# A hybrid GDN and GLA decoder trunk on one core: 32x32 blocks inverted on VectorE in 31 steps in place of 16x16 blocks in 15, decays from one magnitude, early PSUM banks in an order of their own

## The chip, the cores and the metric

The kernel runs on one core of a Trainium2 chip. TensorE (PE) multiplies matrices into PSUM, VectorE (DVE), ScalarE (ACT) and GpSimd (POOL) work elementwise, SyncE (SP) and ACT issue transfers (DMAs). Each engine takes its own instructions in order and waits on semaphores for the others. The metric is the device time of one launch in microseconds, the median over runs.

## The reference, cut to what matters

Two layers over 2048 tokens of width 1024. The first is a gated DeltaNet (GDN) with 8 heads, the second a gated linear attention (GLA) with 4 heads; each is followed by a residual sum and a LayerNorm.

```python
# GDN, per head, in chunks; gc = cumsum of the log decay within a chunk
diff  = gc[..., :, None] - gc[..., None, :]
decay = jnp.where(causal, jnp.exp(jnp.where(causal, diff, 0.0)), 0.0)
A  = jnp.where(strict, einsum('cd,sd->cs', k * beta, k) * decay, 0.0)
uw = triangular_solve(A + eye, concat([v * beta, kb * exp(gc)]))
qk = einsum('cd,sd->cs', q, k) * decay
...
def step(S, inp):                      # over the chunks
    v_new = u_n - w_n @ S
    o = qd_n @ S + qk_n @ v_new
    S = S * gl_n + kd_n.T @ v_new
...
x = layer_norm(DEEP_ALPHA * x + mixer(x), ln_g, ln_b)
```

The change touches how `decay` and the inverse of `A + eye` are made, and how the LayerNorm is staged.

## The kernel before, in words

**Units.** The tokens lie in four groups of 512 (`TG`), each group in four chunks of 128 (`NC`). A unit is one head of one group: 32 GDN units and 16 GLA units. `PHASES` (line 1178) sets their order: GDN group 0, GDN 1, GLA 0, GDN 2, GLA 1, GDN 3, GLA 2, GLA 3. For each unit four functions run (lines 1159 to 1164): `gemms` projects keys, queries, values and the gate; `preps` makes the per-chunk matrices; `chains` runs over the four chunks with the state `S`; `outs` multiplies with the output weights and, at a group's last unit, makes the LayerNorm.

**Projections.** Weights and inputs are split into a high and a low part (fp32r), and three products are summed. In the first units the raw weights (`wraw`) are split on ACT and on POOL (`split`, line 490, from `chunk`), and the pair is written back to DRAM (`wk`); later units load that pair (`wc`, nine buffers).

**A GDN preparation** (`gdn_prep`, line 798). The cumulated decays of a chunk come back from DRAM as rows on all partitions (`Gb`). For each chunk DVE forms their difference to the chunk's own column twice, bounded below by `C_LO` into `D1` and above by `C_UP` into `D2`; ACT takes two exponentials. PE transposes the keys and forms the Gram products (`psc<-kq`); DVE multiplies them with the decays, which gives `A` (in `D1`) and the query matrix (in `D2`). The inverse of the triangular 128x128 matrix is then built up:

- the 16x16 blocks on the diagonal are masked (`W2`), summed to 16 columns (`X`), written to DRAM (`blk`, issued by ACT), and read back so that every partition holds all 16 rows of its block (`Arep`, 512 KB, issued by SP);
- 15 steps on DVE invert all blocks at once, each a product (`Xt<-Arep,X`) and a subtraction (`X<-X,Xt`), the second needing the first and the next step both;
- the blocks are spread to `Tm` and transposed to `U`;
- 16 to 32, 32 to 64 and 64 to 128 are joined on PE, each by one set of matmuls with `A` (`psc<-U,D`) and one with the inverse so far (`psc<-W,Tm`). The join to 32 is made on full 128x128 operands, the later ones on the blocks alone;
- ACT scales the result into `Uf`, which the chain's second product uses (`psh<-Rt,D`).

Each step of the inversion and the lines of this join read as follows (lines 853 to 868, cut):

```python
for q in range(15, 0, -1):
    v.tensor_tensor(xt[:, :, :q], R[:, q, :, :q], X[:, :, q:q + 1].broadcast_to([P, NC, q]), ALU.mult)
    v.tensor_tensor(X[:, :, :q], X[:, :, :q], xt[:, :, :q], ALU.subtract)
...
```

**What sets the order.** The code does not run as it is written. `Recorder.note` records every operation with its dependencies and a rank; `Recorder.place` then lays all of them out with a cost for each (`cost`), a lag until its result can be used, and one clock per engine: of what could go, the lowest rank goes first (chain, preparation, output, projection, LayerNorm, setup), then the earlier recorded. What comes out is each engine's fixed order of instructions; all of them have one line, 364, in the profile. A tile gets its buffer when its first operation is placed, and tiles of one name and one rank get theirs in the order in which they were recorded. So the PSUM banks `psc` of a preparation, three in all, are handed out in recorded order: first the transposes and Gram products of a unit, then those of its joins, then those of the next unit. A dependent operation was taken to be ready 160 ns after the one before it had ended (`LAG`, `SLACK`).

**LayerNorm** (`layer_norm`, line 1145). For each chunk: statistics, then for each half of the 1024 columns two DVE instructions with the gain and the bias (`gb`, four buffers of their own), then a store.

Of the kernel before, what the change touches and what calls it, by code (L numbers as in the profile page):

```python
# [27 lines left out]
BIG = 1.0e30  # L28
# [4 lines left out]
C_ID, C_TRI, C_LO, C_UP, C_BLK, C_LV = 0, 1, 2, 3, 4, 5  # L33
# [3 lines left out]
def shape_constants(np):  # L37
    i = np.arange(P)[:, None]
    j = np.arange(P)[None, :]
    c = np.zeros((P, N_CST, P), np.float32)  # L40
    c[:, C_ID] = i == j
    c[:, C_TRI] = i <= j
    c[:, C_LO] = np.where(j < i, 0.0, BIG)
    c[:, C_UP] = np.where(j >= i, 0.0, -BIG)
    c[:, C_BLK] = (i // 16) == (j // 16)
    for n, s in enumerate(LEVELS[:5]):
        c[:, C_LV + n] = (i // (2 * s) == j // (2 * s)) & (i % (2 * s) < s) & (j % (2 * s) >= s)
    return c.reshape(P, N_CST * P)
# [75 lines left out]
class Recorder:  # L124
# [11 lines left out]
    def note(self, engine, key, name, args, kw, also):  # L136
# [9 lines left out]
        for v in views:  # L146
# [19 lines left out]
            if t not in op.views:  # L166
                op.views.append(t)
                t.left += 1
        for v in also:
# [14 lines left out]
    def cost(self, op, dst, every):  # L184
# [14 lines left out]
        elif key == "d":  # L199
# [3 lines left out]
            if tag == "Arep":  # L203
                op.cost, op.lag = 720, REP_LAG
# [30 lines left out]
    def place(self):  # L235
# [47 lines left out]
        while len(placed) < len(self.ops):  # L283
# [48 lines left out]
            for u in op.users:  # L332
                u.ready = max(u.ready, now + cost if u.deps[op] else end + (100 if u.key == "t" else 0) + SLACK)
# [33 lines left out]
class Recorded:  # L367
# [3 lines left out]
    def __getattr__(self, name):  # L371
        def call(*args, also=(), **kw):
            key = "a" if self.key == "s" and name == "dma_start" else self.key
            self.recorder.note(self.engine, key, name, args, kw, also)
# [3 lines left out]
LAG = 60  # L378
DMA_LAG, REP_LAG, SLACK = 3500, 9000, 100
# [4 lines left out]
def trunk(ctx, tc, x, xT, w_in1, conv, a_log, dt_bias, nw1, w_out1, w_in2, gk_up, gk_b, nw2, w_out2,  # L384
# [51 lines left out]
    id16 = T("id16", [P, 16])  # L436
# [18 lines left out]
    def setup():  # L455
# [11 lines left out]
        v.tensor_reduce(id16[:], ident.rearrange("p (a b) -> p b a", b=16), mybir.AxisListType.X, ALU.add)  # L467
# [34 lines left out]
    def transposes(dst, src_of, n, w=P):  # L502
        for i in range(n):
            pe.transpose(dst[:, i, :], src_of(i), cst[:w, C_ID, :w])
# [239 lines left out]
    def gdn_logits(G, gi):  # L744
# [29 lines left out]
        gc, gl = T("gc", [P, 2, H1, NC], 2), T("gdec", hn, 2)  # L774
# [3 lines left out]
        s.activation(gl[:], gl[:], AF.Exp)  # L778
        eg = T("eg", [P, 2, H1, NC], 2)
# [7 lines left out]
        G.update(beta=beta, gc=gc, gdec=gl, eg=eg, rows=rows)  # L787
# [10 lines left out]
    def gdn_prep(u):  # L798
        h, G = u.h, u.G
        beta, gc, eg = G["beta"][:, h, :], G["gc"][:, 0, h, :], G["eg"]  # L800
# [4 lines left out]
        for n in range(NC):  # L805
            v.scalar_tensor_tensor(D1[:, n], Gb[:, n], gc[:, n:n + 1], C(C_LO), ALU.subtract, ALU.max)
            v.scalar_tensor_tensor(D2[:, n], Gb[:, n], gc[:, n:n + 1], C(C_UP), ALU.subtract, ALU.min)
        s.activation(D1[:], D1[:], AF.Exp, scale=-1.0)
        s.activation(D2[:], D2[:], AF.Exp)
        s.activation(Gb[:], Gb[:], AF.Exp)  # L810
        kq = u.kq
        qd = T("qd", [P, NC, P], 2)
        v.tensor_tensor(qd[:], kq[:, 1], Gb[:], ALU.mult)
        ss, r, qn = small("ss", 2 * NC), small("rr", NC), small("qn", NC)
        kd = T("kd", [P, NC, P], 2)
        for m in range(2 if u.by_tok else 1):
            d = PS("c", [P, NC, P])
            transposes(d, lambda n: kq[:, m, n], NC)
# [13 lines left out]
        for n in range(0, NC, 2):  # L832
            d = PS("c", [P, 2, 2 * P])
            for i in range(2):
                mm(d[:, i, :], kq[:, 0, n + i], kq[:, :, n + i, :])
            for i in range(2):
# [4 lines left out]
        Tm, U, W2 = T("Tm", [P, NC, P]), T("U", [P, NC, P]), T("W2", [P, NC, P])  # L841
        X = T("X", [P, NC, 16])
        v.tensor_tensor(W2[:], A[:], bc(C(C_BLK), 1, NC), ALU.mult)
        v.tensor_reduce(X[:], W2[:].rearrange("p n (b j) -> p n j b", j=16), mybir.AxisListType.X, ALU.add)
        blk = T(f"blk_{u.at}", [P, NC * 16], p=dr)
        acts.dma_start(blk[:], flat(X[:]))
        R = T("Arep", [P, 16, NC, 16])
        sync.dma_start(R[:].rearrange("p s n j -> p (s n j)"),
                            bc(blk[:].rearrange("(b s) n -> b (s n)", b=8), 1, 16))
        X = T("X", [P, NC, 16])  # L850
        xt = T("Xt", [P, NC, 16])
        g.tensor_copy(X[:], bc(id16[:], 1, NC))
        for q in range(15, 0, -1):
            v.tensor_tensor(xt[:, :, :q], R[:, q, :, :q], X[:, :, q:q + 1].broadcast_to([P, NC, q]), ALU.mult)
            v.tensor_tensor(X[:, :, :q], X[:, :, :q], xt[:, :, :q], ALU.subtract)
        v.tensor_tensor(Tm[:].rearrange("p n (b j) -> p n b j", j=16), bc(X[:], 2, 8),
                        bc(C(C_BLK).rearrange("p (b j) -> p b j", j=16), 1, NC), ALU.mult)
        v.transpose(flat(U[:]), flat(Tm[:]))
        Uh, Wh = later_half(U[:], 16), halves(W2[:, :, :P // 2], 16)
        d = halves(PS("c", [P, NC, P // 2]), 16)  # L860
        for n in range(NC):
            mm(d[:, n], A[:, n], Uh[:, n])
        v.tensor_tensor(Wh, d, bc(later_half(C(C_LV + 4), 16), 1, NC), ALU.mult)
        d = halves(PS("c", [P, NC, P // 2]), 16)
        for n in range(NC):
            mm(d[:, n], Tm[:, n], Wh[:, n])
        v.tensor_tensor(Uh, Uh, d, ALU.subtract)
        v.transpose(flat(Tm[:]), flat(U[:]))
# [21 lines left out]
    def gla_prep(u):  # L890
# [3 lines left out]
        ab, xm = T("Gb", [P, TG]), T("W2", [P, TG])  # L894
# [12 lines left out]
        near = T("Arep", [P, NC, 2 * P])  # L907
# [186 lines left out]
    def outs(u):  # L1094
# [9 lines left out]
        if end:  # L1104
            wo = {e: load_wo(spec, ("xh", "xl")) for e, spec in enumerate(u.wo_specs())}
            gb = load_gb(u)
        for e, n in [(e, n) for n in range(NC) for e in range(2)] if end else [(e, n) for e in range(2) for n in range(NC)]:
# [3 lines left out]
            if final and not n and not end:  # L1111
                rec.rank = R_LN
                gb = load_gb(u)
                rec.rank = R_OUT
# [7 lines left out]
            if final:  # L1122
                if not end:
# [95 lines left out]
```

## Time and profile before

| | us |
|---|---|
| median of 3 runs | 3043.78 (3040.22 to 3046.16) |
| the profiled execution | 3042.14 |
| its span, first to last instruction | 3040.3 |
| PE busy | 2961.3 (97%) |
| PE weight loads busy | 2470.7 (81%) |
| DVE busy | 2099.5 (69%) |
| ACT busy | 1183.6 (39%) |
| POOL busy | 508.9 (17%) |

An engine's busy time is the time in which it had an instruction under way; 1.8 us of the execution lie outside the span. A group's row gives line, engine, operation, what it writes and from what, shapes and count, then busy time and mean of one in ns, then the idle time before it and what ended that. A wait's row gives who waited, for whom, us in total, times, and the longest. TensorE's granted clock was 0.994 in the mean. An fp32 matmul stands as two records.

### The profile page before, as it was taken

The page shows a single profiled execution, that of the slowest core. Times are in us where ns is not written, and L with a number is a line of the kernel's source. Part 1 is how long each engine was busy: PE and PEld are TensorE (multiplying, and loading weights), DVE is VectorE, ACT ScalarE, POOL GpSimd, SP SyncE. Part 2 cuts the span into 40 slices and gives each one's busy share as a digit, 9 for nine tenths or more (in the row PEclk, how much of TensorE's full clock was granted, in tenths as well). Part 3 has the DMA queues.
Part 4 walks back from the last instruction along what each step waited for, and adds up shares of the span by engine and source line. Part 5 has one row for each costly group of instructions (what it writes and reads, how often), then busy time and mean ns, then how long its engine had stood idle before and what let it go on. Part 6 is the DMA issues. An engine that isn't in the chain of part 4 may idle for free. (4 is left out here: it accounts for less than half of the span.)

```text
span 3040.3 us, 47938 instructions
## 1 busy us (share of the span) xinstructions
PE 2961.3 (97%) x16684; PEld 2470.7 (81%) x16684; DVE 2099.5 (69%) x4730; ACT 1183.6 (39%) x3009; POOL 508.9 (17%) x848
## 2 busy tenths in 40 slices
PE   8999999999999999999999999999999999999997
PEld 6777778778888888878888888888888888888886
DVE  6877787866776696576677668448667676655755
ACT  5444444533323455332332344333333334433431
POOL 5443333410000233210000000001001000000000
PEclk9999999999999999999999999999999999999998
DMA  6666666764556557785454556667454545766754
GB/s 189 179 202 193 212 219 197 248 216 139 149 154 174 173 181 255 237 268 165 143 150 150 178 177 199 220 222 257 136 154 147 159 150 177 253 198 218 236 177 146
DMA packets 455778, 577.33 MB, mean 190 GB/s; under 512 B 40640, under 2 KB 387008, under 8 KB 443504
## 3 DMA queue, kind: packets, MB, share of 16 engines
q1 hardware_dynamic: 441520, 556.37, 58.3%
q10 hardware_dynamic: 14016, 17.90, 2.0%
q8 instruction: 131, 2.15, 0.3%
q14 instruction: 111, 0.91, 0.1%
HBM read 446.94 MB, written 127.21 MB: 189 GB/s over the span
## 5 line engine op out<-in xcount | busy, mean ns | idle before, releaser
L364 PE MATMUL psg<-xh,wc 128*128 128x512 f32 x3936 | 1337.8, 407 | 19.9 <-DMA wc<-wk 6.9
L364 PEld LDWEIGHTS psg<-xh,wc 128*128 128x128 f32 x3936 | 735.0, 189 | 181.2 <-POOL wc L364 9.6
L364 PE MATMUL psg<-xl,wc 128*128 128x512 f32 x1968 | 799.5, 407 | 0.3
L364 PE MATMUL pso<-wo,oth 128*128 128x512 f32 x1472 | 489.5, 406 | 12.2 <-DVE y L364 12.1
L364 PEld LDWEIGHTS psg<-xl,wc 128*128 128x128 f32 x1968 | 372.3, 189 | 75.4 <-DVE xl L364 1.9
L364 DVE SCALAR_TENSOR_TENSOR y<-pso,z,y 128x512 f32<-128x512 f32 x368 | 274.8, 747 | 182.0 <-PE pso L364 171.2
L364 POOL TENSOR_TENSOR wc<-wraw,wc 128x256 fp32r<-128x256 f32 (+1 forms) x336 | 288.6, 875 | 428.0 <-ACT wc L364 383.5
L364 DVE SCALAR_TENSOR_TENSOR acc<-pb,taps,acc 128x512 f32<-128x512 f32 x384 | 302.9, 793 | 53.9 <-ACT acc L364 49.9
L364 PEld LDWEIGHTS pso<-wo,oth 128*128 128x128 f32 x1472 | 262.6, 189 | 71.1 <-DVE y L364 21.1
L364 PE MATMUL pso<-wo,otl 128*128 128x512 f32 x736 | 292.8, 398 | 0.0
L364 PE MATMUL psg<-wc,xh 128*128 128x256 f32 (+1 forms) x1344 | 267.9, 291 | 8.4 <-ACT wc L364 3.9
L364 PEld LDWEIGHTS psg<-wc,xh 128*128 128x128 f32 x1344 | 216.0, 189 | 20.1 <-ACT wc L364 4.7
L364 ACT ACTIVATE th<-psg 128x512 f32<-128x512 f32 (+1 forms) x170 | 94.6, 572 | 302.7 <-PE psg L364 297.9
L364 PE MATMUL psg<-wc,xl 128*128 128x256 f32 (+1 forms) x672 | 190.2, 289 | 0.0
L364 ACT CAST wc<-wraw 128x256 fp32r<-128x256 f32 (+1 forms) x336 | 126.5, 405 | 103.1 <-DMA wraw<-in_w_in 86.0
L364 PEld LDWEIGHTS pso<-wo,otl 128*128 128x128 f32 x736 | 138.7, 188 | 29.9 <-DVE otl L364 1.1
L364 ACT COPY pb<-psg 128x512 f32<-128x512 f32 x128 | 74.8, 584 | 214.0 <-PE psg L364 202.5
L364 ACT ACTIVATE D<-D 128x512 f32<-128x512 f32 x160 | 98.1, 628 | 127.6 <-DVE D L364 121.2
L364 POOL COPY halo<-pb 128x3 f32<-128x3 f32 x128 | 36.8, 287 | 638.8 <-ACT pb L364 637.0
L364 DVE SCALAR_TENSOR_TENSOR sg<-th,psg 128x512 f32<-128x512 f32 (+1 forms) x106 | 67.0, 633 | 110.4 <-ACT th L364 100.9
L364 POOL TENSOR_SCALAR z<-ssq 128x4 f32<-128x4 f32 x44 | 16.3, 370 | 752.9 <-ACT junk L364 728.2
L364 ACT ACTIVATE sq<-psc 128x256 f32<-128x256 f32 x172 | 65.5, 382 | 163.3 <-PE psc L364 161.6
(192 smaller groups left out, 4608.0 us busy)
## 6 DMA issues: line engine op xcount, KB each, us to landing
wc<-wk SPq DMA_DIRECT2D x856, 256.0 KB
wo<-wok SPq DMA_DIRECT2D x70, 1024.0 KB
wk<-wc SPq DMA_DIRECT2D x272, 256.0 KB
wraw<-in_w_in SPq DMA_DIRECT2D x336, 128.0 KB
wok<-wo SPq DMA_DIRECT2D x24, 1024.0 KB
wc<-wk SPq DMA_DIRECT2D x80, 272.0 KB
Arep<-blk SPq DMA_DIRECT2D x32, 512.0 KB
woraw<-in_w_out SPq DMA_DIRECT2D x48, 256.0 KB
```

What stands on the lines that cost most here:

```text
L364: tc.keep_in_program_order(op.call(*[real(a) for a in op.args], **{k: real(a) for k, a in op.kw.items()}))
```

## The change

What it does:

- The diagonal blocks are 32x32: 31 steps of two instructions on DVE for 15, and the join from 16 to 32 on PE goes away, with its two DVE instructions, its mask and one transpose on DVE. ACT copies the blocks to `X0` in place of DVE's mask and sum. The block is written whole (`blk`) and as its first 16 columns (`blkq`), and read back in two transfers: rows 16 to 31 (1 MB), and rows 0 to 15 as far as they are needed (512 KB).
- The decays come from one magnitude: ACT takes `Abs(Gb - gc)` once per chunk (bias from a negated copy `ngc`) and one exponential for both uses; a product with the triangle makes `D2` from it. DVE's eight bounded differences per unit go.
- The preparation's first part (transposes, Gram products) has a rank of its own, `R_EARLY`, behind the preparation's. Its PSUM banks are so handed out in an order of their own, and it can be placed ahead of the joins of the unit before.
- In `place`, an operation of DVE that needs one of DVE is ready 35 ns after that one has ended (`DRAIN`). The lag of `Arep` is counted from 8500 ns and its size.
- LayerNorm takes the statistics of all four chunks first, then the first half of the columns of each, then the second. Its gains and biases are loaded half by half, after the first statistics, into buffers that the raw output weights (`woraw`) or the inputs (`xraw`) use otherwise.

The diff's core:

```diff
-    c[:, C_LO] = np.where(j < i, 0.0, BIG)
-    c[:, C_UP] = np.where(j >= i, 0.0, -BIG)
-    c[:, C_BLK] = (i // 16) == (j // 16)
+    c[:, C_BLK] = (i // 32) == (j // 32)
...
-                u.ready = max(u.ready, now + cost if u.deps[op] else end + (100 if u.key == "t" else 0) + SLACK)
+                u.ready = max(u.ready, now + cost if u.deps[op] else end - LAG + DRAIN if u.key == op.key == "v" else
+                              end + (100 if u.key == "t" else 0) + SLACK)
...
         for n in range(NC):
-            v.scalar_tensor_tensor(D1[:, n], Gb[:, n], gc[:, n:n + 1], C(C_LO), ALU.subtract, ALU.max)
-            v.scalar_tensor_tensor(D2[:, n], Gb[:, n], gc[:, n:n + 1], C(C_UP), ALU.subtract, ALU.min)
+            s.activation(D1[:, n], Gb[:, n], AF.Abs, bias=ngc[:, n:n + 1])
         s.activation(D1[:], D1[:], AF.Exp, scale=-1.0)
-        s.activation(D2[:], D2[:], AF.Exp)
         s.activation(Gb[:], Gb[:], AF.Exp)
+        v.tensor_tensor(D2[:], D1[:], bc(C(C_TRI), 1, NC), ALU.mult)
...
+        rec.rank = R_EARLY
...
         A = D1
...
-        v.tensor_tensor(W2[:], A[:], bc(C(C_BLK), 1, NC), ALU.mult)
-        v.tensor_reduce(X[:], W2[:].rearrange("p n (b j) -> p n j b", j=16), mybir.AxisListType.X, ALU.add)
-        blk = T(f"blk_{u.at}", [P, NC * 16], p=dr)
-        acts.dma_start(blk[:], flat(X[:]))
-        R = T("Arep", [P, 16, NC, 16])
-        sync.dma_start(R[:].rearrange("p s n j -> p (s n j)"),
-                            bc(blk[:].rearrange("(b s) n -> b (s n)", b=8), 1, 16))
+        rec.rank = R_PREP
+        own = T("X0", [P, 32 * NC])
+        for r0 in range(0, P, 32):
+            r = slice(r0, r0 + 32)
+            s.copy(own[r].rearrange("p (j n) -> p n j", n=NC), A[r, :, r])
+        late, early = (T(f"{k}_{u.at}", [P, 32 // m * NC], p=dr) for m, k in ((1, "blk"), (2, "blkq")))
+        acts.dma_start(late[:], own[:])
+        acts.dma_start(early[:], own[:, :16 * NC])
+        R = T("Arep", [P, 3 * 16 * 16 * NC])
+        n = 16 * 32 * NC
+        sync.dma_start(R[:, :n], bc(late[:].rearrange("(b s) n -> b (s n)", b=4)[:, n:], 1, 32))
+        sync.dma_start(R[:, n:], bc(early[:].rearrange("(b s) n -> b (s n)", b=4)[:, :n // 2], 1, 32))
...
-        for q in range(15, 0, -1):
-            v.tensor_tensor(xt[:, :, :q], R[:, q, :, :q], X[:, :, q:q + 1].broadcast_to([P, NC, q]), ALU.mult)
-            v.tensor_tensor(X[:, :, :q], X[:, :, :q], xt[:, :, :q], ALU.subtract)
+        for q in range(31, 0, -1):
+            at = (q - 16) * 32 * NC if q >= 16 else n + q * 16 * NC
+            row = R[:, at:at + q * NC].rearrange("p (j n) -> p j n", n=NC)
+            v.tensor_tensor(xt[:, :q], row, bc(X[:, q], 1, q), ALU.mult)
+            v.tensor_tensor(X[:, :q], X[:, :q], xt[:, :q], ALU.subtract)
...
-        for n in range(NC):
-            mm(d[:, n], A[:, n], Uh[:, n])
-        v.tensor_tensor(Wh, d, bc(later_half(C(C_LV + 4), 16), 1, NC), ALU.mult)
-        d = halves(PS("c", [P, NC, P // 2]), 16)
-        for n in range(NC):
-            mm(d[:, n], Tm[:, n], Wh[:, n])
-        v.tensor_tensor(Uh, Uh, d, ALU.subtract)
-        v.transpose(flat(Tm[:]), flat(U[:]))
...
+        if u.last and not end:
+            rec.rank = R_LN
+            for e in range(2):
+                rec.after = stats[0][0].of.given
+                gb = load_gb(u, [e])
+                rec.after = None
+                for n in range(NC):
+                    layer_norm(u, n, ys[n], e, *stats[n], gb)
...
-R_CHAIN, R_PREP, R_OUT, R_GEMM, R_LN, R_SETUP = range(6)
+R_CHAIN, R_PREP, R_EARLY, R_OUT, R_GEMM, R_LN, R_SETUP = range(7)
```

How the instructions move, at three places. On PE, the joins of the first unit; `psg<-xh,wc` is a projection of a later unit, `U` and `W` the operands of the joins, `D` holds `A`. Before:

```order
L364 MATMUL psg_111<-xh_127,wc_137 128x512
L364 MATMUL psc_168<-U_200,D_0_178 128x64 x4
L364 MATMUL psg_110<-xh_124,wc_143 128x512
L364 MATMUL psg_110<-xl_132,wc_143 128x512
L364 MATMUL psg_110<-xh_124,wc_143 128x512
L364 MATMUL psg_111<-xh_128,wc_138 128x512
L364 MATMUL psg_111<-xl_136,wc_138 128x512
L364 MATMUL psc_169<-W_0_201,Tm_199 128x64 x4
```

And now:

```order
L364 MATMUL psg_109<-xh_126,wc_138 128x512
L364 MATMUL psc_167<-U_201,D_0_179 32x32 x8
L364 MATMUL psg_109<-xh_127,wc_137 128x512
L364 MATMUL psg_109<-xl_135,wc_137 128x512
L364 MATMUL psg_109<-xh_127,wc_137 128x512
L364 MATMUL psc_168<-W_0_202,Tm_200 32x32 x8
```

The two runs of four 128x64 matmuls are gone, and the first join is that on 32x32 blocks.

Also on PE, the transposes (`cst,kq`) and Gram products (`kq` 128x256) of the second unit, whose keys and queries are `kq_116`. Before they stand behind the first unit's last join (`W,Tm` 64x64):

```order
L364 MATMUL psg_109<-xh_122,wc_140 128x512
L364 MATMUL psg_109<-xl_130,wc_140 128x512
L364 MATMUL psc_169<-W_0_201,Tm_199 64x64 x4
L364 MATMUL psc_168<-cst_63,kq_116 128x128 x4
L364 MATMUL psg_109<-xh_122,wc_140 128x512
L364 MATMUL psc_169<-kq_116 128x256 x2
L364 MATMUL psh_215<-Rt_216,D_0_178 128x256
```

Now they stand here, more than a hundred rows ahead of that join:

```order
L364 MATMUL psg_109<-xh_126,wc_138 128x512
L364 MATMUL psg_109<-xh_127,wc_139 128x512
L364 MATMUL psc_168<-cst_63,kq_116 128x128 x4
L364 MATMUL psc_167<-kq_116 128x256 x2
L364 MATMUL psg_109<-xl_135,wc_139 128x512
L364 MATMUL psg_109<-xh_127,wc_139 128x512
```

The second unit's products have moved from behind the first unit's joins to before its inversion.

On DVE, steps of the inversion in the third unit, from its first on, before, with other work of DVE between: `acc` is the short convolution, `otl` and `sq` belong to the outputs.

```order
L364 TENSOR_TENSOR X_202<-X_202,Xt_205 128x4x15
L364 SCALAR_TENSOR_TENSOR acc_156<-pb_152,taps_65,acc_156 128x512
L364 TENSOR_TENSOR otl_212<-og_214,oth_210 128x512
L364 TENSOR_TENSOR sq_232<-psc_167,cst_63 128x512
L364 TENSOR_TENSOR Xt_205<-Arep_204,X_202 128x4x14
L364 SCALAR_TENSOR_TENSOR acc_156<-pb_152,taps_65,acc_156 128x512
L364 TENSOR_TENSOR X_202<-X_202,Xt_205 128x4x14
L364 SCALAR_TENSOR_TENSOR acc_156<-pb_152,taps_65,acc_156 128x512
```

And now, from the third of 31 steps on (`Rt` and `og` belong to the chain of the unit before):

```order
L364 TENSOR_TENSOR og_217<-psc_168,sg_158 128x2x128
L364 TENSOR_TENSOR X_207<-X_207,Xt_208 128x116
L364 SCALAR_TENSOR_TENSOR Rt_219<-psh_218,s_1_199,vt_114 128x256
L364 TENSOR_TENSOR Xt_208<-Arep_206,X_207 128x112
L364 TENSOR_TENSOR X_207<-X_207,Xt_208 128x112
L364 TENSOR_TENSOR Xt_208<-Arep_206,X_207 128x108
L364 TENSOR_TENSOR X_207<-X_207,Xt_208 128x108
L364 TENSOR_TENSOR Xt_208<-Arep_206,X_207 128x104
```

The steps stood singly with other work between; now they stand in pairs and longer runs, and the chain of the unit before runs beside them.

## What the change will do to the time

> **What bounds the kernel now.** First the page's busy shares, then the same by stage (one group of 512 tokens is eight GDN units, one per head; GLA units lie between). The columns are stretch, length, then busy us and instructions of PE, PEld, DVE, ACT, POOL, the granted clock, DMA share and rate.
>
> ```profile
> PE 2961.3 (97%) x16684; PEld 2470.7 (81%) x16684; DVE 2099.5 (69%) x4730; ACT 1183.6 (39%) x3009; POOL 508.9 (17%) x848
> ```
> ```profile
> 0.00:640.00 640.00, 606.11 (x3227) 485.62 (x3228) 498.59 (x1050) 304.06 (x832) 260.01 (x374) 0.99 0.66 206
> 1360.00:1800.00 440.00, 439.25 (x2426) 362.84 (x2425) 300.94 (x744) 147.82 (x392) 35.39 (x90) 1.00 0.52 160
> 2100.00:2540.00 440.00, 440.00 (x2456) 364.24 (x2455) 300.60 (x749) 151.91 (x402) 35.81 (x92) 1.00 0.53 163
> ```
>
> The late GDN stages (1360 to 1800, 2100 to 2540) have PE busy 439.25 and 440.00 of 440 us: PE sets their length. The first stage (0 to 640) has 33.9 us of idle PE, with DVE at 498.59 of 640 (78%) and POOL at 260.01. What PE waited for, first there, then from 1360 to 1800:
>
> ```profile
> PE pso L364 <- DVE y L364: 8.1, 11, 1.9
> PE psg L364 <- DVE acc L364: 7.2, 7, 2.7
> PE psg L364 <- POOL wc L364: 3.9, 9, 1.2
> ```
> ```profile
> PE psg L364 <- DVE sg L364: 0.8, 1, 0.8
> ```
>
> 19.2 us of the first stage's waits end on DVE or POOL; in the later stage 0.8 us in all does, and no wait for weights is there. So work taken from PE shortens the kernel, and DVE is what can take some back, early on.
>
> Then one unit's preparation, in the timeline (start, length):
>
> ```profile
> 2322.34 0.33 ACTq L364 DMA_DIRECT2D blk<-X  x1
> 2327.34 0.62 SPq L364 DMA_DIRECT2D Arep<-blk  x1
> 2335.93 0.22 DVE L364 TENSOR_TENSOR Xt<-Arep,X 128x60 f32<-128x60 f32 x1
> ...
> 2357.07 0.17 DVE L364 TENSOR_TENSOR Xt<-Arep,X 128x4 f32<-128x4 f32 x1
> ```
> ```profile
> 2369.74 0.68 PE L364 MATMUL psc<-W,Tm 64*64 64x64 f32 x8
> 2370.35 0.65 PE L364 MATMUL psc<-cst,kq 128*128 128x128 f32 x4
> ...
> 2371.93 0.59 PE L364 MATMUL psh<-Rt,D 128*128 128x256 f32 x2
> ...
> 2379.68 0.33 ACTq L364 DMA_DIRECT2D blk<-X  x1
> ```
>
> The last level (2369.74) is followed at once by the next unit's transposes (2370.35) and by the chain that uses the result (2371.93); the next unit's blocks are written at 2379.68, 57.3 us after this unit's. The preparations run one behind the other.
>
> **The change, part by part.** The sum is made against the profiled execution: 3042.14 us, its span 3040.3. The median of the runs shown is 1.6 us above it.
>
> (a) PE loses the level that joined 16 to 32: four matmuls by A and four by the inverse, in every one of 32 units, two records each. Two places, and what starts behind them:
>
> ```profile
> 797.61 1.00 PE L364 MATMUL psc<-U,D 128*128 128x64 f32 x8
> 798.42 0.71 PE L364 MATMUL pso<-wo,oth 128*128 128x512 f32 x2
> ...
> 799.66 1.00 PE L364 MATMUL psc<-W,Tm 128*128 128x64 f32 x8
> 800.47 0.48 PE L364 MATMUL pso<-wo,otl 128*128 128x512 f32 x1
> ...
> 801.80 0.59 PE L364 MATMUL psc<-U,D 128*32 128x32 f32 x16
> ```
>
> From start to next start a run of eight takes 0.81 us, its 1.00 us being modelled to an end that overlaps the next. I take the starts: 2 x 0.81 x 32 = 51.8 us; by the durations it would be 64, which would count the overlap. Nothing is added on PE. Since its stages are full, this is on the path: -51.8. The level's latency, 4.2 us (797.61 to 801.80), goes from the preparation too.
>
> (b) DVE loses these, and gets 62 inversion instructions a unit for 30:
>
> ```profile
> L364 DVE SCALAR_TENSOR_TENSOR D<-Gb,gc,cst 128x128 f32<-128x128 f32 x256 | 82.6, 369 | 4.7 <-PE psh L364 3.7 <-DMA Gb<-gcT 0.9
> ...
> L364 DVE TENSOR_REDUCE X<-W 128x64 f32<-128x512 f32 x32 | 33.0, 1032 | 0.3
> ...
> L364 DVE STREAM_TRANSPOSE Tm<-U 128x512 f32<-128x512 f32 x32 | 22.7, 709 | 0.8
> ...
> L364 DVE TENSOR_TENSOR W<-D,cst 128x512 f32<-128x512 f32 x32 | 22.4, 699 | 0.1
> ...
> L364 DVE TENSOR_TENSOR W<-psc,cst 128x256 f32<-128x256 f32 x32 | 13.5, 421 | 24.0 <-PE psc L364 23.7
> L364 DVE TENSOR_TENSOR U<-U,psc 128x256 f32<-128x256 f32 x32 | 13.4, 419 | 23.3 <-PE psc L364 23.2
> ```
>
> Removed per unit: 8 x 0.369 + 1.032 + 0.709 + 0.699 + 0.421 + 0.419 = 6.2 us. Added: one 512-wide product with the triangle, 0.7 us by the row of W<-D. The inversion's price differs by stage; these rows hold its products Xt alone (stretch, length, DVE busy and count):
>
> ```profile
> 0.00:640.00 640.00, 80.19 (x270) 0.99 0.66 206
> 2100.00:2540.00 440.00, 45.36 (x240) 1.00 0.53 163
> ```
>
> That is 0.297 us each early and 0.189 us late; the subtractions I price alike. The mean width doubles from 32 to 64 elements, and 56 elements cost 0.05 us in the rows above (0.22 at 60, 0.17 at 4), so 0.03 us each is added. Late: 62 x 0.219 = 13.6 us for 30 x 0.189 = 5.7, so with the rest +2.4 us a unit; in stages that have 140 us of 440 without DVE work, and PE hardly waits for it, I cost this at nothing. Early (nine units): 62 x 0.327 = 20.3 for 8.9, +5.9 a unit, 53 us together. DVE would be busy 552 of 640 - 9 x 1.6 = 625 us, 88% for 78%. Why the early ones are dearer:
>
> ```profile
> 442.78 3.09 POOL L364 TENSOR_TENSOR wc<-wraw,wc 128x256 fp32r<-128x256 f32 x4 [3.35 <-ACT wc L364]
> ...
> 444.58 0.66 DVE L364 TENSOR_TENSOR Xt<-Arep,X 128x52 f32<-128x52 f32 x1
> ...
> 445.97 0.21 DVE L364 TENSOR_TENSOR Xt<-Arep,X 128x48 f32<-128x48 f32 x1
> ```
>
> While POOL splits weights, a step takes 0.66 us, and 0.21 us as soon as it has stopped. The Trainium skill, SBUF — State Buffer, section "SBUF: two separate sides", has a rule that speaks against this change: a vector instruction with two SBUF inputs and a GpSimd instruction that reads SBUF exclude each other for a whole instruction. By it the steps would be hit in proportion to POOL's share of the stretch; 260 of 640 us at 0.45 us a hit is an estimate of 0.18 us per step, 25 us a unit for my 20, and 42 us more of DVE in the stage.
>
> What of these 53 us PE sees no row shows. From below: nothing, since steps are not what PE waits for above (y, acc and wc are). From above: the stage's idle DVE time halves, 141 to 73 us; if the 19.2 us of waits grow as it shrinks, they become 37, +18. Both ends are equally near, so I take +9.
>
> (c) ACT loses one exponential of 512 and gets four magnitudes of 128 and four copies of 32x128 blocks, and another write is issued:
>
> ```profile
> L364 ACT ACTIVATE D<-D 128x512 f32<-128x512 f32 x160 | 98.1, 628 | 127.6 <-DVE D L364 121.2 <-DVE lnmv L364 4.0 <-PE psg L364 2.1
> ...
> L364 ACT ACTIVATE D<-U,brk 128x128 f32<-128x128 f32 x128 | 40.9, 391 | 0.9
> ```
>
> At 0.39 us for each of the eight, 0.63 back and 0.33 for the issue: +2.8 us a unit on an engine busy 39%. Nothing; its cover is ACT's free 60%, and if the copies came late the inversion would start 1.6 us later.
>
> (d) Arep grows from 512 KB to 1.5 MB in two DMAs. Before, 8.6 us went from issue (2327.34) to the first step. Three times that, 26 us, bounds the whole from above, but the first steps need only the first megabyte. On SP the second DMA waits for its block's write, and weight loads are queued behind both. SP's own waits:
>
> ```profile
> SPq L364 <- PE psg L364: 1130.2, 637, 8.9
> ```
>
> SP mostly waits for buffers that PE frees, so loads go out early, and no weight was waited for from 1360 to 1800. Nothing, with 2 us a unit (64 us) as the far end if that lead is eaten.
>
> (e) The early PSUM banks in an order of their own, and vector steps placed closer: the next unit's transposes and Gram products no longer stand behind this unit's last level. That takes the longer inversion off the row of preparations: 13.6 - 5.7 = 7.9 us longer, 4.2 us of level gone. It may also free some early waits: 0, at best the whole 19.2 us.
>
> (f) LayerNorm in halves: the instruction counts stay, the gains and biases land in buffers shared with weights, and their issue waits for the first statistics, with the next unit's loads behind it on SP. Seven groups with a wait of a microsecond would be 7 us; I take 0, by the same lead.
>
> Sum: 3042.1 - 51.8 + 9 = 2999.3; with the 1.6 us to the median, 3001 us.
>
> **The rivals.**
> - *The waits do not grow* (0.34): PE saves its 51.8 us and the freed order saves some early waits, as y and acc are short steps that a vector engine with 12% to spare still serves. Against it: DVE at 88%. 2980 to 2992 us; all 19.2 us saved would be 2971.
> - *Half-late inversions* (0.13): the early steps make PE wait 2 to 4 us a unit, 18 to 36 us: 3010 to 3028.
> - *The inversion becomes the early bound, slower* (0.05): the steps cost 0.327 - 0.219 = 0.108 us more than in quiet, 62 of them 6.7 us a unit, and if PE's in-order queue reaches the next level before them each time, nine units lose 60 us: 3052. It outweighs the saving from 5.8 us a unit on. For it: steps now stand in pairs without other work between. Against: before, 3.2 us of the same excess a unit left no wait for U among the early waits.
> - *Weights late behind Arep* (0.04): from 1.6 us of PE wait a unit on there is no gain; at 2 us, 3054. Against it the SP row.
> - *PE's busy time is no bound, no gain* (0.04): the preparations' row sets the 57.3 us, and what PE loses becomes idle: 3042. The Trainium skill, Perfetto Trace Analysis, section "Identifying the Most-Contended Engine", holds that matmul busy time misjudges headroom and asks for the share of the weight loads; here that is 364.24 of 440 us. Against it: a run of 0.81 us is followed at once by the next start, and hardly a wait is left in the late stages (0.8 us) that an earlier operand would shorten.
>
> **The numbers.** The forecast, 2993 to 3010 us, has 0.40. A measurement of this kernel can tell about 0.2% (6 us) from no change. Slower by more: 0.05, of the inversion rival 0.03 and of the weights rival 0.02, the rest of both ending below 3038. Same: the no-gain case, 0.04. Faster: what is left, 0.91. For 8 in 10 the range takes in the forecast, nearly all of the first two rivals and with them the unknowns of (d) and (f): 2975 to 3026.
>
> **What would show it.** In the profile after: no psc 128x64 matmuls by U and Tm; PE still 440 of 440 in late stages, now some 13 us shorter per group; Xt near 0.33 us early and 0.22 us late; DVE near 88% before 630 us; PE's early waits on y and acc near 30 us. An early wait of psc for U or W, or of psg for wc behind Arep, would prove a rival; PE idle in the late stages would prove the reasoning wrong from its start.

## The result and the profile after

The change makes the kernel slower: 3476.39 us (median of 4 runs, 3468.62 to 3481.28) against 3042.49 in the same rounds, a ratio of 1.1424 with an interval of 1.1410 to 1.1439. The forecast was 3001 us. The profiled execution took 3474.92 us, with a span of 3472.7 and a granted clock of 0.933 in the mean.

The page's busy shares of the changed kernel:

```profile
PE 2992.4 (86%) x16172; PEld 2464.3 (71%) x16172; DVE 2207.5 (64%) x5374; ACT 1263.2 (36%) x3233; POOL 506.4 (15%) x848
```

PE ran 512 matmul records fewer. They are those of the join to 32, which is gone as forecast; a group of the joins has the forms 32 and 64 alone:

```profile
L364 PE MATMUL psc<-W,Tm x768: 191/191/367, 132.3 to 2969.5; 32*32 32x32 f32 x128, 64*64 64x64 f32 x64
```

PE was yet busy 31 us longer, and its idle time went from 79.0 us (3040.3 - 2961.3) to 480.3 (3472.7 - 2992.4). These two make the 432 us by which the span grew. By stage (stretch, length, then PE, PEld, DVE, ACT, POOL, the granted clock, DMA share, rate):

```profile
0.00:640.00 640.00, 504.04 (x2473) 394.88 (x2474) 415.36 (x983) 268.62 (x729) 211.99 (x304) 0.90 0.55 174
1360.00:1800.00 440.00, 384.03 (x2140) 319.91 (x2139) 280.48 (x660) 166.78 (x426) 79.56 (x124) 0.95 0.65 208
2100.00:2540.00 440.00, 397.82 (x2263) 339.56 (x2262) 271.35 (x646) 153.34 (x360) 27.94 (x57) 0.95 0.62 200
```

PE was to stay at 440 of 440 in the late stages and DVE to come near 88% in the first. Neither holds: DVE has 65% there (415 of 640). No engine is the bound, so the waits must tell. PE's, then one row of ACT's and one of DVE's (us in total, times, longest):

```profile
PE psg L364 <- DMA wc<-wk: 204.9, 25, 19.9
PE psg L364 <- ACT wc L364: 55.0, 7, 14.4
PE psh L364 <- DVE S L364: 51.4, 12, 9.5
PE pso L364 <- DVE y L364: 38.9, 18, 9.8
PE psh L364 <- ACT wt L364: 31.5, 7, 16.0
PE psh L364 <- DVE Rt L364: 23.5, 2, 14.0
```
```profile
ACT wc L364 <- DMA wraw<-in_w_in: 191.0, 42, 19.6
```
```profile
DVE Xt L364 <- DMA Arep<-blk: 173.8, 22, 11.4
```

Two chains come out of one place. PE waits 204.9 us for loaded weights, and 55.0 for ACT, which itself stands on raw weights not yet loaded. The waits that end on DVE (S, y, Rt) are no work of DVE's: it stands at the first step of an inversion 22 times until `Arep` lands, and what is queued behind that step on its engine waits too.

One unit in the timeline (start, length; in brackets the idle time before and what ended it):

```profile
1065.93 0.33 ACTq L364 DMA_DIRECT2D blk<-X  x1
...
1068.87 0.56 SPq L364 DMA_DIRECT2D Arep<-blk  x1
...
1069.53 0.55 SPq L364 DMA_DIRECT2D Arep<-blkq  x1
...
1070.70 16.37 SPq L364 DMA_DIRECT2D wc<-wk  x4
...
1077.40 0.40 PE L364 MATMUL psg<-xh,wc 128*128 128x512 f32 x1
...
1094.57 0.80 PE L364 MATMUL psg<-xh,wc 128*128 128x512 f32 x1 [16.78 <-DMA wc<-wk]
```
```profile
1101.46 0.28 DVE L364 TENSOR_TENSOR Xt<-Arep,X 128x124 f32<-128x124 f32 x1
```

SP issued the weights that PE lacks at 1070.70, 7 us before PE ran out: the lead that the prediction counted on was there. They came 24 us later. The trace has 16 semaphore updates for this load, one for each part that landed: twelve by 1076.17, the last four at 1090.04, 1091.68, 1093.72 and 1094.53. The four late ones of `Arep`'s second load stand at 1089.37, 1091.01, 1093.05 and 1093.84, each 0.7 us ahead of one of those. So a quarter of the weights went behind `Arep`, part by part. SP was held as well: its third issue of weights behind `Arep` (1072.98) took 9.28 us, the fourth 4.76, where in e1 below none took over 1.6. What the DMA engines did while only `Arep` was under way, from the windows of three kernels (here with PE alone: PE busy, clock, DMA share, rate), the changed kernel first, then the kernel before, then e1 below:

```profile
1076.50:1079.50 3.00, 1.30 (x6) 1.00 0.27 74
```
```profile
2269.10:2271.10 2.00, 2.00 (x12) 1.00 0.50 134
```
```profile
1625.00:1628.00 3.00, 3.00 (x15) 1.00 1.06 232
```

The changed kernel moves the three times larger tile with a quarter of the 16 engines, where the kernel before used half of them. The source of the load has its blocks outermost: eight of 16 rows before, four of 32 now. The Trainium skill, DMA: Bandwidth & Descriptors, section "Why a DMA increments its semaphore by 16 and not by 1", says that the outermost size that is not 1 sets on how many engines a transfer is spread, the largest number up to 16 that divides it on both sides. By that eight and four are what one should have expected, and the shares of 0.50 and 0.27 agree.

### The profile page after: what moved, and what is told of

It reads as the page before. It is cut to its first block, busy times and chain, and to the rows that moved or that the text cites. A ratio compares the mean times of both kernels' runs of the same rounds, so it can differ in the third digit from the quotient of the medians.

```text
span 3472.7 us, 47799 instructions
## 1 busy us (share of the span) xinstructions
PE 2992.4 (86%) x16172; PEld 2464.3 (71%) x16172; DVE 2207.5 (64%) x5374; ACT 1263.2 (36%) x3233; POOL 506.4 (15%) x848
## 5 line engine op out<-in xcount | busy, mean ns | idle before, releaser
L364 PE MATMUL psg<-xh,wc 128*128 128x512 f32 x3936 | 1365.7, 414 | 261.2 <-DMA wc<-wk 195.5
L364 PEld LDWEIGHTS psg<-xh,wc 128*128 128x128 f32 x3936 | 753.4, 193 | 439.3 <-DMA wc<-wk 204.8
L364 PE MATMUL psg<-xl,wc 128*128 128x512 f32 x1968 | 813.1, 414 | 0.2
L364 PE MATMUL pso<-wo,oth 128*128 128x512 f32 x1472 | 500.7, 414 | 40.7 <-DVE y L364 38.9
L364 PEld LDWEIGHTS psg<-xl,wc 128*128 128x128 f32 x1968 | 380.9, 194 | 78.9 <-DVE xl L364 1.5
L364 DVE TENSOR_TENSOR Xt<-Arep,X 128x124 f32<-128x124 f32 (+30 forms) x992 | 235.8, 238 | 196.9 <-DMA Arep<-blk 173.8
L364 DVE TENSOR_TENSOR X<-X,Xt 128x124 f32<-128x124 f32 (+30 forms) x992 | 234.7, 237 | 23.7
L364 DVE SCALAR_TENSOR_TENSOR S<-S,eg,psh 128x256 f32<-128x256 f32 x128 | 61.2, 478 | 173.2 <-PE psh L364 172.8
```

What stands on the lines that cost most here:

```text
L364: tc.keep_in_program_order(op.call(*[real(a) for a in op.args], **{k: real(a) for k, a in op.kw.items()}))
```

## The experiments

Three theories. **Width**: on four engines `Arep` takes long, and the weights, spread over all 16, wait for their share on these four. **Volume**: 1.5 MB in place of 0.5 is too much however spread. **Placement**: the early rank, or a planner that was told too short a lag, puts weights behind `Arep`. Times stand against the kernel before on the same chip, 3041 to 3043 us.

**e1, full width.** Each load as four, one for each 32 partitions:

```diff
-        sync.dma_start(R[:, :n], bc(late[:].rearrange("(b s) n -> b (s n)", b=4)[:, n:], 1, 32))
-        sync.dma_start(R[:, n:], bc(early[:].rearrange("(b s) n -> b (s n)", b=4)[:, :n // 2], 1, 32))
+        for part, src in ((R[:, :n], late[:].rearrange("(b s) n -> b (s n)", b=4)[:, n:]),
+                          (R[:, n:], early[:].rearrange("(b s) n -> b (s n)", b=4)[:, :n // 2])):
+            for b in range(4):
+                sync.dma_start(part[b * 32:(b + 1) * 32, :], src[b:b + 1, :].broadcast_to([32, src.shape[1]]))
```

> The changed kernel, with each of its two Arep loads issued as four, one per block of 32 partitions, so that the slowest dimension of each source is the 32 copies and no longer the 4 blocks; bytes, steps and ranks stay. Width theory (the load runs on 4 of the 16 DMA engines, busy share 0.25 in the trace, and weights queue behind it on those): the load lands within 8 us, the gaps of 10 to 17 us go, 2985 to 3020 us. Volume theory (1.5 MB in place of 512 KB is what holds the weights up): still over 3300 us. Placement theory (the new ranks and lags put DVE and SP in front of rows that cannot be there yet): still over 3300 us.

3036.1 us, ratio 0.9983 (0.9971 to 0.9994). With this one edit the whole loss is gone, 440 us, and bytes and steps are what they were: width is shown. Of 936 weight loads, 96 took over 10 us from issue to landing in the changed kernel, none here; the two loads of `Arep` took 20 and 25 us there (medians), 6 and 7 for each part here. Its page, two stages and four of PE's waits:

```profile
PE 2927.2 (96%) x16172; PEld 2416.5 (80%) x16172; DVE 2211.9 (73%) x5374; ACT 1261.3 (42%) x3233; POOL 510.3 (17%) x848
```
```profile
0.00:640.00 640.00, 595.75 (x3021) 469.45 (x3022) 516.81 (x1218) 326.30 (x892) 264.52 (x376) 0.98 0.71 217
1360.00:1800.00 440.00, 430.27 (x2331) 350.92 (x2331) 326.63 (x915) 167.93 (x450) 33.48 (x85) 0.99 0.63 184
```
```profile
PE psg L364 <- DMA wc<-wk: 26.8, 14, 5.2
PE pso L364 <- DVE y L364: 11.8, 18, 1.6
PE psg L364 <- ACT acc L364: 10.6, 9, 2.9
...
PE psc L364 <- DVE U L364: 4.9, 5, 2.7
```

This is the kernel that the prediction had in mind, but at 3036, not 3001, and above the 2985 to 3020 of the width theory too; that is taken up by e5 and those after it.

**e2, the kernel before on four engines.** Its 512 KB as two loads of four blocks each:

```diff
-        sync.dma_start(R[:].rearrange("p s n j -> p (s n j)"),
-                       bc(blk[:].rearrange("(b s) n -> b (s n)", b=8), 1, 16))
+        for k in range(2):
+            sync.dma_start(R[k * 64:(k + 1) * 64].rearrange("p s n j -> p (s n j)"),
+                           bc(blk[k * 64:(k + 1) * 64, :].rearrange("(b s) n -> b (s n)", b=4), 1, 16))
```

> The kernel before, with its 512 KB Arep load issued as two of 4 blocks each in place of one of 8 blocks; bytes, steps and placement nearly as before. Width theory: the DMA busy share in the load falls from about 0.5 to 0.25, the load takes about twice as long (9 to 10 us from its first to its last packet, for 4.5), weights come later and the steps start 4 to 5 us later: 3070 to 3200 us. Volume theory and placement theory: no more bytes and no other placement, 3035 to 3055 us.

3056.26 us, ratio 1.0049 (1.0029 to 1.0068). The load did go narrow. A window with little but this load under way (PE busy, clock, DMA share, rate):

```profile
890.50:893.50 3.00, 3.00 (x15) 1.00 0.28 101
```

The loss is less than width expected: a quarter of the engines costs 15 us where 512 KB go over them, and 440 where 1.5 MB do. It takes both, the narrow transfer and the larger tile.

**e3 and e4, placement.** `R_EARLY` made the same as `R_PREP`; and `REP_LAG` 22000 for 8500:

> The changed kernel with the early part of the preparation back in the preparation's own rank, so that PSUM banks are handed out in recorded order as before. Width theory and volume theory: over 3400 us, the load is as slow as it was. Placement theory, if the early rank is what did it: below 3150 us.

> The changed kernel, with the planner told that Arep's rows come 22 us and their size later in place of 8.5 us and their size; the transfers are as they were. Placement theory (the too short lag makes DVE wait in its queue for rows): DVE's waits for Arep go and the time falls below 3060 us. Width theory: DVE's waits for Arep go, but the weights behind it stay late, 3200 to 3450 us with PE still waiting over 100 us for wc. Volume theory: as width.

3619.55 us, ratio 1.1896 (1.1865 to 1.1927), and 3526.99, 1.1595 (1.1567 to 1.1623). Both slower than the change itself, e4 also than any of its expectations. Placement is out: without the early rank it is worse, and a planner that is told of the slow load gains nothing. In e4 DVE never waits for `Arep` any more, and PE's waits for `S` fall from 51.4 to 1.4 us, but those for weights rise to 280.1. So the late weights alone are enough for the loss; DVE need not stand for it.

**e7, issued by ACT.** Both loads on ACT's queue (`acts.dma_start` for `sync.dma_start`), still four blocks outermost:

> The changed kernel with both loads of the repeated rows issued by ACT's queue in place of SP's, still on four engines. If the weights lose their time by standing behind these loads in SP's own queue (queue), they pass them now: most of the 440 us goes, 3050 to 3150. If they lose it because the four engines that carry the repeated rows are shared by all queues (engines), a weight load needs those four too, and 250 us or more stays: 3290 to 3480. The first step's wait for the repeated rows stays at 25 us or more in both.

3469.86 us, ratio 1.1401 (1.1379 to 1.1423): the loss stays. Two of its waits:

```profile
PE psg L364 <- DMA wc<-wk: 121.2, 38, 10.9
```
```profile
DVE Xt L364 <- DMA Arep<-blk: 236.7, 24, 14.7
```

PE waits less for weights (204.9 in the changed kernel), DVE more for the repeated rows (173.8), and the time is the same. SP is free now: 4 of its weight issues took over 2 us, 59 in the changed kernel. Yet 102 weight loads were over 10 us under way, for 96, and the repeated rows took 21 and 27 us from issue to landing (medians). So it is not SP's queue but the four engines that both need.

**e8, the kernel before on all 16.** Its load as eight of 16 partitions each.

> The kernel before with its load of the repeated rows cut into eight DMAs of 16 partitions, so that all 16 engines carry its 512 KB. Width: the 10.6 us of waits for weights shrink a little, 3034 to 3042, ratio 0.997 to 1.000. If eight engines were wide enough for 512 KB: no change, 3040 to 3043. If seven more issues a unit on SP cost something: above 3045.

3046.18 us, ratio 1.0015 (1.0004 to 1.0026): no gain, if anything a loss. Eight engines were wide enough for 512 KB; whether the seven more issues cost the 5 us was not tested.

Now the 35 us between e1 and the forecast. The busy and idle time of PE in the profiled executions, worked out from span and busy time of each page:

| | time of the runs, us | PE busy | PE idle |
|---|---|---|---|
| before | 3041 | 2961.3 | 79.0 |
| e13, join left out | 2994.6 | 2908.2 | 78.9 |
| e9, few bytes, few steps | 3020.3 | 2918.6 | 94.6 |
| e1, full width | 3036.1 | 2927.2 | 108.2 |
| after | 3476.4 | 2992.4 | 480.3 |

(Of e13 and e9 the busy times are in the rows below; the idle time is the span less these: 2987.1 and 3013.2.)

```profile
PE 2908.2 (97%) x16172; PEld 2414.3 (81%) x16172; DVE 2064.9 (69%) x4634; ACT 1184.2 (40%) x3009; POOL 513.5 (17%) x848
```
```profile
PE 2918.6 (97%) x16172; PEld 2416.3 (80%) x16172; DVE 1987.8 (66%) x4350; ACT 1264.0 (42%) x3233; POOL 501.5 (17%) x848
```

**e5, e6, e9: bytes and steps.** e5 loads four late and eight early rows of each block (`R[:, :n // 4]`, and `n // 4` more), e6 runs `range(15, 0, -1)` for `range(31, 0, -1)`, e9 does both; all on e1.

> e1_full_width with a third of the bytes: of each block only four late rows and eight quarter rows are loaded (512 KB a unit in place of 1.5 MB, still one DMA for each 32 partitions), and the steps read these rows again and again, so it leaves out the other rows of the inverse; the number and the shapes of the steps stay. Volume: the waits of the matmuls for weights (wc<-wk 26.8 us in e1_full_width, 10.6 before) fall to about 10 us, and what follows them too: 3036 goes to 3008 to 3022, near the forecast. DVE load (the early steps themselves make PE wait): the time stays at 3032 to 3038 and the waits for y, acc and U stay. If both hold part, 3022 to 3032.

> e1_full_width with 15 of the 31 steps (it leaves out the 16 widest), all 1.5 MB loaded as before. 32 DVE instructions of about 0.3 us a unit go, some 9 us a unit, 300 us of DVE in all. DVE load: PE's waits for DVE (y 11.8, acc 5.2, U 4.9, kq 4.1 us in e1_full_width) shrink, 3008 to 3022. Volume: the time stays within 6 us of e1_full_width, 3030 to 3040, and the waits for weights stay near 27 us.

> e5_third_of_bytes and e6_half_the_steps in one kernel: 512 KB of repeated rows a unit on all engines, and 15 of the 31 steps (it leaves out the 16 widest steps, and most rows of the rest). Neither volume nor DVE load is then above the kernel before. If each of the two alone made up for the other in e5 and e6 (either-or): most of the 42 us comes through, 3000 to 3015. If neither is the cause, and the residue is the order of the work or ACT's part (order/ACT): 3030 to 3045 again.

3037.12 us, ratio 0.9989 (0.9979 to 0.9999); 3044.33, 1.0018 (1.0008 to 1.0028); 3020.3, 0.9932 (0.9918 to 0.9947). Neither alone gives anything (e6 is even 8 us slower than e1), both together 16 us. So volume alone and DVE load alone both fell, and "either-or" holds for a third of what it forecast. In e5 the weights were waited for less, and other waits came up:

```profile
PE pso L364 <- DVE y L364: 14.6, 20, 2.7
PE psg L364 <- DMA wc<-wk: 14.4, 9, 3.6
PE psg L364 <- ACT acc L364: 11.3, 9, 3.5
```

In e1 these were 11.8, 26.8 and 10.6 us (above). (For the kernel before, PE's waits for weights are 9.5 us in the trace, where the expectations have 10.6.) Why one of the two is enough to hold the other's gain was not found.

**e13, the join left out of the kernel before**, with its eight matmuls and their vector work, nothing in its place.

> The kernel before with the join of 16 to 32 left out and nothing put in its place (eight matmuls and their vector work a unit go; blocks of 16 in place of 32 are inverted, so the result lacks the join). PE bound as the prediction had it: the whole 51.8 us come through, 2984 to 2996, perhaps some more since DVE gets lighter too. If waits for weights and vector work come up as PE gets lighter (a second bound close behind): 3005 to 3030. PE no bound: 3036 to 3043.

2994.55 us, ratio 0.9846 (0.9831 to 0.9860), 46.6 us less. PE busy falls by 53.1 us and its idle time does not move (table), in an execution that was the fastest of the five: what PE sheds comes through, as the prediction reckoned.

**e15, the LayerNorm in halves alone** on the kernel before, and **e17**, on e1, its halves ranked `R_OUT` for `R_LN`.

> The kernel before with only the LayerNorm in halves, its gains and biases in the weights' buffers and issued behind the first statistics. The prediction put 0, at worst 7 us: 3040 to 3049. If it takes back a good part of the saving: 3049 to 3065.

> e1_full_width with the halves of the LayerNorm ranked as the output products in place of behind the projections. If what the halves cost is that they come late and hold the weights' buffers: 3022 to 3032. If it is the wait on SP's queue for the statistics: 3034 to 3045.

3054.65 us, ratio 1.0037 (1.0026 to 1.0047): 13 us lost by the medians, 8 to 14 by the interval, more than the 7 that were forecast as the worst. e17 is slower still, 3065.01, 1.0073 (1.0060 to 1.0086), beyond both its expectations. That the halves cost is shown; by what is not, since the profiled execution of e15 was its fastest, with a span of only 3043.5 us.

**e10 and e14, the decays as before**, on e1 and on e9: the two bounded differences for each chunk back on DVE, for ACT's magnitude.

> e1_full_width with the decays made as before: two subtractions with a limit on DVE for each block and a second exponential of 512 on ACT, in place of four magnitudes on ACT and one product on DVE; the result is the same. ACT (its added work makes PE wait for acc, wc and xh): ACT's waits go from 10.6 us for acc back to about 3, and the time to 3018 to 3028. Order: 3030 to 3042. DVE load: 72 us more on DVE, so slower, 3040 to 3055.

> e9_few_bytes_few_steps (a third of the bytes, 15 of the 31 steps, so it leaves out the same) with the decays made as before. If ACT's added work holds the remaining 20 us to the forecast: 2998 to 3010. If it is the order of the work: 3015 to 3028. If DVE counts: 3022 to 3035.

3038.25 us, ratio 0.9987 (0.9975 to 0.9998), as e1; but 3009.57, 0.9897 (0.9883 to 0.9911), 11 us less than e9. PE's waits for `acc` from ACT, 9.8 us in e9, are gone in e14. So the added work on ACT costs 11 us where the wide inversion does not. In e10 these waits fall too, from 10.6 us to 3.5, but those for `y` rise from 11.8 to 18.4, and nothing is won.

**e11 and e12, the order at full width**: e1 without the early rank, and with `DRAIN` 160 for 35.

> e1_full_width with the next unit's transposes and Gram products ranked as the rest of the preparation. On four engines this cost 143 us. If the early rank only hides a late start of the inversion: at full width 8 to 60 us slower than 3036. If the early rank pushes other work late at full width (order): 3010 to 3028.

> e1_full_width where the planner reckons 160 ns between a vector instruction and the next one that needs it, as before, in place of 35 ns, so that it puts other work between the steps again. If the closely packed steps hold up DVE's other work (order): 3010 to 3028. If other work between the steps only lengthens the inversion: 3040 to 3070. If neither: 3033 to 3039.

3116.37 us, ratio 1.0237 (1.0224 to 1.0250), and 3033.9, 0.9973 (0.9963 to 0.9984). The early rank is worth 80 us here. Without it PE is busy 29 us longer (2955.8) and idle 50 us longer (158.1). Some 11 of these 50 stand at the joins, where the prediction had looked (`psc` for `U`, 4.9 us in e1):

```profile
PE psc L364 <- DVE U L364: 16.3, 7, 5.0
```

Its waits for weights rise by as much (37.0 for 26.8), and so do those for `y` (22.2 for 11.8). The closer steps are worth nothing that can be told. e12 is the fastest of the kernels that leave nothing out, 0.3% below the kernel before.

**e16 and e18, LayerNorm (and decays) as before on e1.** The gains' own buffers no longer fit beside the larger `Arep`, so they went into those of the transposed input.

> e1_full_width with the LayerNorm as before (each tile of 128 tokens whole, right after its last product), its four gains and biases in the buffers of the transposed input, since buffers of their own no longer fit beside the larger repeated rows. If the 13 us of e15 add to the rest: 3018 to 3028. If the wide inversion and the weights take them anyway: 3032 to 3040.

> e16 with the decays made as before too, so that only the wide inversion at full width, the early rank and the planner's numbers are left of the change. Additive: 3008 to 3020. Not additive, as e10 had it for the decays: as e16 within 6 us.

3384.73 us, ratio 1.1123 (1.1109 to 1.1138), and 3407.25, 1.1197 (1.1173 to 1.1222). The edit brought a loss of its own. The largest of PE's waits in e16 is for `y` (100.7 us), the next this:

```profile
PE psg L364 <- ACT xh L364: 58.1, 12, 14.0
```

The first gains were loaded into the inputs' buffers at 375 us and used only from 589 us on, so the next group's inputs had fewer. That this makes up the loss was not shown. These two tell nothing of the LayerNorm; whether its 13 us can be had at full width stays open.

## Why the prediction was wrong, point by point

**(d) is the step that failed.** "Nothing, with 2 us a unit as the far end" rested on SP issuing the weights early, so that they would be there in time. SP did issue them 7 us before PE ran out. But the load itself took 24 us, where a weight load took 3.8 us in the kernel before (median from issue to landing). The step priced when loads are issued and how long `Arep` takes, and left out how long the loads beside it take. For `Arep` itself the 26 us were about right: in the unit above the first megabyte had landed 20.1 us after its issue, all of it after 25.0. That was partly luck. "Three times that" takes the old rate for granted; by the rates in the windows above, the transfer alone goes from 3.9 us (512 KB at 134 GB/s) to 21 (1.5 MB at 74 GB/s), five times. (The first step came only at 1101.46, since DVE was by then itself waiting 19.2 us for PE.) The rival "weights late behind Arep" named the right place, at 2 us a unit with a chance of 0.04; measured are 401 us more idle time, 12.5 a unit. The row "SP waits for PE" that stood against it was no evidence: it tells when a load is issued, not how long it is under way. The number that would have warned was in the trace of before, the DMA share of 0.50 while `Arep` was alone, and in the diff, `b=8` to `b=4`.

**A second loss came with the first.** 31 of the 432 us stand in no wait. The same 16172 matmuls took 2992.4 us here and 2927.2 in e1, 65 us more. By the clock records of the two traces PE was busy at half clock for 183.0 us here and for 50.2 in e1; half of the difference is 66 us, so the clock accounts for it. The clock in the gap shown above and behind it (ahead of it, it was 1.00):

```profile
1079.50:1082.00 2.50, 0.00 (x0) 0.87 0.23 72
...
1085.00:1090.00 5.00, 0.00 (x0) 0.50 0.39 130
...
1095.00:1098.00 3.00, 3.00 (x13) 0.50 0.03 12
1098.00:1102.00 4.00, 4.00 (x19) 0.95 0.00 0
```

PE stopped at 1077.80 and came back at 1094.57. The record has half clock from 1081.35 to 1098.41: from 3.6 us after the stop to 3.8 us after the return. The Trainium skill, TensorE: Matmul & The Clock Gate, section "What's actually happening", has the clock halved after an idle window of about 3.4 us and given back after one of work; the rows agree. The prediction had no term for this.

**(a) was right**: 51.8 us forecast, 53.1 of PE's busy time and 46.6 of the runs' time measured (e13). By that the rival "PE's busy time is no bound", with no gain, is out. The rule of the Trainium skill that stood beside it (Perfetto Trace Analysis, section "Identifying the Most-Contended Engine") is not tested by this, since the weight loads' busy time fell as much (2470.7 to 2414.3 us). Of the other rivals, the inversion did not become the early bound: PE waits 4.9 us for `U` in all of e1.

**(b) had the load too high, and what PE sees of it too low.** The products Xt of e1, early and late:

```profile
0.00:640.00 640.00, 156.79 (x553) 0.98 0.71 217
2100.00:2540.00 440.00, 109.30 (x492) 0.99 0.62 184
```

That is 0.284 us for 0.327 forecast, and 0.222 for 0.219; DVE stood at 81% in the first stage (516.81 of 640), not 88. The excess of early over late steps is 0.06 us, a third of the 0.18 that the two-sides rule of the Trainium skill (SBUF — State Buffer, section "SBUF: two separate sides") came to in that estimate. Yet steps and bytes together cost 16 us (e9 to e1), for 9.

**(c) was costed at nothing and came to 11 us** beside a narrow inversion, to nothing beside the wide one (e14, e10). ACT's free 60% was no cover for work that PE's inputs queue behind: PE's waits for `acc` from ACT went from 3.2 us before to 10.6 in e1.

**(e) was right in kind**: without the order of its own the longer inversion costs 80 us (e11).

**(f) was costed at 0, at worst 7, and cost 13** (e15).

Summed as measured, each from another pair of kernels: -46.6 (e13) + 13.5 (e15) + 10.7 (e14 to e9) + 15.8 (e9 to e1) = -6.6, and e1 measures -5.3. The last two terms lead from e14 to e1 by themselves, so what the sum tests is that the first two, -33.1, come out at e14, which measures -31.6. Each variant is also laid out anew by `place`, and its whole order moves with it: e6 lost 8 us on e1 by leaving steps out. So the single terms are good to some 10 us, and what they are put down to is argued where no wait shows it. Had the load been wide, the change would have been worth 5 us, not 42, since three covers were taken for complete that were not. The lost width then adds 440.

## What to carry to other kernels

When a change reshapes a transfer, work out from its outermost size on how many DMA engines it goes, before and after, and read the DMA share while it is alone. Then price the loads behind it, and not only the transfer itself: an early issue is no cover when the load takes 24 us in place of 4. Here a narrow transfer of 1.5 MB held up the loads that needed the same engines, whether SP or ACT issued it; cutting it by partitions gave the width back. And terms put at little because an engine has time to spare add up: here three, costed at 9 us together, took back some 40 of 47.

## What the runs showed of the hardware that was not expected

The clock falls after gaps well below 3.4 us too. Two places of e1, with the window of the gap first:

```profile
70.00:73.20 3.20, 0.27 (x2) 1.00 0.90 189
73.20:76.20 3.00, 3.00 (x10) 0.75 0.96 217
76.20:80.00 3.80, 3.80 (x14) 0.75 1.01 341
...
113.00:115.70 2.70, 0.07 (x1) 0.99 0.96 229
115.70:119.00 3.30, 3.26 (x36) 0.50 1.00 307
119.00:123.00 4.00, 4.00 (x16) 0.57 0.51 169
```

PE stood for 2.9 and 2.7 us. The clock column is a mean over the window; the record itself has only full and half clock: half from 74.69 on for 3.4 us in the first place, though PE was back at 73.20, and from 115.65 on for 6.8 us in the second. PE was busy through both, so that is 1.7 and 3.4 us of work lost. The first 130 us of the kernel before and of e1:

```profile
0.00:130.00 130.00, 117.03 (x577) 90.41 (x578) 94.41 (x186) 65.21 (x180) 65.89 (x96) 1.00 0.60 181
```
```profile
0.00:130.00 130.00, 114.43 (x538) 89.22 (x539) 91.23 (x197) 68.70 (x184) 65.50 (x94) 0.95 0.65 192
```

In the same 130 us e1 gets through 39 records fewer. Of e1's 19 us of PE busy time above e13's, for as many matmuls (2927.2 and 2908.2), 10 go the same way: PE was busy at half clock for 50.2 us in e1 and for 29.9 in e13. What the other 9 are stays open. In the two places above, a PE wait cost 1.6 and 2.3 times what the wait's row shows.
